# Two more steps in the size ramp of a channel shuffle: 4, 8, 16, 24, 32, then eleven tiles of 38 KB, 10 KB last

## The chip, the cores and the metric

The kernel runs on one core of a Trainium2 chip. The time is device microseconds (us) of that core for one execution. Most executions agree within 0.3%. A run is classed slow when it lies over 1.5% above the fastest run of the same kernel; only the other runs, classed fast, are compared. The profile is one execution. Its span, the time between its first and its last recorded instruction, is about 1.8 us shorter than the time of the same run. All sizes of tiles below are in KB for each of the 128 partitions: a "38 KB tile" is 128 rows of 38 KB, 4,864 KB in all.

## The reference

```python
x = np.random.randn(16, 64, 64, 256).astype(np.float32)   # 67.1 MB
groups = 8

def reference(x, groups):
    batch, h, w, c = x.shape
    x = x.reshape(batch, h, w, groups, c // groups)
    x = x.transpose(0, 1, 2, 4, 3)          # swap the two halves of the channel index
    return x.reshape(batch, h, w, c)
```

It is a permutation inside each group of 256 channels. Nothing is calculated: 67.11 MB are read and 67.11 MB are written.

## The kernel before

The 512 KB that each partition handles are cut into tiles. A tile is loaded in one DMA issued by SyncE, permuted by one copy on VectorE (DVE), and stored in one DMA issued by ScalarE. There are three input and two output buffers, so the copy of tile k waits until the store of tile k-2 has landed, and the load of tile k+3 is issued when the copy of tile k is done.

```python
_SIZES = [4, 8, 16] + [38] * 12 + [28]
_IN_BUFS = 3
_OUT_BUFS = 2
# ... (setting up, pools)
    for q in _SIZES:
        in_tile = in_pool.tile([P, biggest * c], F32, name="in_tile")
        nc.sync.dma_start(out=in_tile[:, : q * c], in_=rows(x_flat, first, q))
        out_tile = out_pool.tile([P, biggest * c], F32, name="out_tile")
        nc.vector.tensor_copy(
            out=out_tile[:, : q * c].rearrange("p (i j g) -> p i j g", j=CPG, g=G),
            in_=in_tile[:, : q * c].rearrange("p (i g j) -> p i j g", g=G, j=CPG),
        )
        nc.scalar.dma_start(out=rows(out_flat, first, q), in_=out_tile[:, : q * c])
        first += P * q
```

## Time and profile before

| | before |
|---|---|
| time, median of 3 runs (range) | 316.21 us (316.15 to 316.38) |
| span of the profiled run | 314.7 us |
| bytes moved | 134.22 MB, 427 GB/s over the span |
| load queue, store queue: share of the 16 DMA engines | 49.8%, 49.4% |
| DVE busy | 119.2 us (38%) |

The table says at once that transfers, not copies, fill the time. The view of the waits gives the opposite impression if it is read alone (columns: who waited for what, us in total, times, longest):

```profile
DVE out_tile L49 <- DMA out_dram<-out_tile: 175.9, 14, 14.6
```

DVE waits 176 us for stores to free an output buffer.

### The profile page before, as it was taken

What the parts mean: (1) busy time and instruction counts of PE and PEld (TensorE: products, weight loads), DVE (VectorE), ACT (ScalarE), POOL (GpSimd) and SP (SyncE); (2) the same over time, 40 slices, a digit from 0 to 9 for tenths busy, and PEclk for the clock granted to TensorE, in tenths of its full rate; (3) what the DMA queues carried; (4) which work ended last, traced back from release to release, by engine and by line L of the source; (5) the groups of instructions that cost most, each with busy time, mean ns of one, the idle gap of its engine ahead of it and who ended that gap; (6) DMA issues with size and microseconds to landing.
All of it is one profiled execution on the core that took longest, in us unless ns stands there. A gap on an engine that the chain in (4) does not pass through costs nothing.

```text
span 314.7 us, 133 instructions
## 1 busy us (share of the span) xinstructions
DVE 119.2 (38%) x16; POOL 0.2 (0%) x4
## 2 busy tenths in 40 slices
DVE  3040645505506407407308209109109019046620
POOL 0000000000000000000000000000000000000000
DMA  8999999999999999999999999999999999999997
GB/s 308 452 398 454 413 419 466 396 475 396 455 415 445 425 430 440 425 445 415 455 396 470 401 465 406 460 411 460 411 460 411 460 411 455 428 395 454 455 418 306
DMA packets 4608, 134.22 MB, mean 427 GB/s; under 512 B 512, under 2 KB 512, under 8 KB 768
## 3 DMA queue, kind: packets, MB, share of 16 engines
q1 hardware_dynamic: 2304, 67.11, 49.8%
q10 hardware_dynamic: 2304, 67.11, 49.4%
HBM read 67.11 MB, written 67.11 MB: 427 GB/s over the span
## 4 chain that ended last, share of the span: by engine, by line
DMA 75%; DVE 20%; issue 0%; SPq 0%; DVEq 0%
DMA out_dram<-out_tile 74%; DVE out_tile L49 20%; DMA in_tile<-in_x_dram 2%; SPq L47 0%; DVEq L49 0%
## 5 line engine op out<-in xcount | busy, mean ns | idle before, releaser
L49 DVE COPY out_tile<-in_tile 128x9728 f32<-128x9728 f32 (+4 forms) x16 | 119.2, 7449 | 181.4 <-DMA out_dram<-out_tile 175.9
L71 POOL MEMSET const-bfloat16-1.0<- 128x1 bf16 x1 | 0.1, 102 | 0.0
L71 POOL MEMSET const-uint8-127<- 128x1 uint8 x1 | 0.1, 102 | 0.0
L71 POOL MEMSET const-float32-1.0<- 128x1 f32 x1 | 0.1, 99 | 0.0
L71 POOL MEMSET const-float32-0.0<- 128x1 f32 x1 | 0.1, 98 | 0.2 <-issue 0.2
## 6 DMA issues: line engine op xcount, KB each, us to landing
in_tile<-in_x_dram SPq DMA_DIRECT2D x12, 4864.0 KB, 46.8
out_dram<-out_tile ACTq DMA_DIRECT2D x12, 4864.0 KB, 37.0
in_tile<-in_x_dram SPq DMA_DIRECT2D x1, 3584.0 KB, 43.8
out_dram<-out_tile ACTq DMA_DIRECT2D x1, 3584.0 KB, 13.3
in_tile<-in_x_dram SPq DMA_DIRECT2D x1, 2048.0 KB, 11.0
out_dram<-out_tile ACTq DMA_DIRECT2D x1, 2048.0 KB, 26.7
in_tile<-in_x_dram SPq DMA_DIRECT2D x1, 1024.0 KB, 5.4
out_dram<-out_tile ACTq DMA_DIRECT2D x1, 1024.0 KB, 25.8
```

The lines of the kernel that those rows point to most:

```text
L49: nc.vector.tensor_copy(out=out_tile[:, : q * c].rearrange("p (i j g) -> p i j g", j=CPG, g=G), in_=in_tile[:, : q * c].rearrange("p (i g ...
L71: nc = _bacc.Bacc("TRN2", target_bir_lowering=False, num_devices=1)
```

## The change

The intent is a smoother start: between the tile of 16 KB and those of 38 KB come steps of 24 and 32 KB, so that small stores do not have to share the DMA engines with loads of 38 KB, and output buffers come free sooner. The last tile shrinks from 28 to 10 KB, which also shortens the last copy and the last store.

```diff
-_SIZES = [4, 8, 16] + [38] * 12 + [28]
+_SIZES = [4, 8, 16, 24, 32] + [38] * 11 + [10]
```

## The prediction

> **What bounds the kernel now.** I read the page first (shares of the span, the 40 slices, the DMA queues), then the chain that ended last, the timeline of the copies, and last a table of windows cut at the starts of the copies. The page says that only one engine computes, and that it works little more than a third of the time, while the DMA engines are busy in every slice but the first and the last:
>
> ```profile
> span 314.7 us, 133 instructions
> DVE 119.2 (38%) x16; POOL 0.2 (0%) x4
> ...
> DMA  8999999999999999999999999999999999999997
> ...
> q1 hardware_dynamic: 2304, 67.11, 49.8%
> q10 hardware_dynamic: 2304, 67.11, 49.4%
> HBM read 67.11 MB, written 67.11 MB: 427 GB/s over the span
> ```
>
> Loads (q1) and stores (q10) take 49.8% and 49.4% of the sixteen engines' time: 99.2% together. The chain alone could mislead. It alternates a copy with the wait for a store that frees an output buffer, and so puts 20% of the span on DVE:
>
> ```profile
> DMA 75%; DVE 20%; issue 0%; SPq 0%; DVEq 0%
> ```
>
> A copy on this chain would cost time only if the DMA engines ran dry meanwhile. The windows say whether they do. Columns: window, its length, DVE busy, POOL busy, clock, DMA share, GB/s.
>
> ```profile
> 0.00:1.50 1.50, 0.00 (x0) 0.20 (x4) 1.00 0.00 0
> 1.50:5.00 3.50, 0.91 (x1) 0.00 (x0) 1.00 0.96 346
> 5.00:12.00 7.00, 2.19 (x2) 0.00 (x0) 1.00 0.99 394
> 12.00:20.36 8.36, 0.00 (x1) 0.00 (x0) 1.00 1.11 477
> 20.36:34.50 14.14, 3.90 (x2) 0.00 (x0) 1.00 0.98 415
> 34.50:51.03 16.53, 8.75 (x1) 0.00 (x0) 1.00 1.02 436
> ...
> 294.00:304.00 10.00, 6.54 (x1) 0.00 (x0) 1.00 1.01 436
> 304.00:311.00 7.00, 0.00 (x0) 0.00 (x0) 1.00 1.02 438
> 311.00:314.70 3.70, 0.00 (x0) 0.00 (x0) 1.00 0.38 163
> ```
>
> From 1.5 us on no window has a DMA share below 0.96 until the drain, not even the one that holds the last copy (294 to 304). Long packets are counted in one window whole, so 477 and 415 are one rate, about 438, seen twice. The packet records agree: the sum of all packets' times over 16 engines is 311.9 us, and the first packet starts at 1.8 us and the last ends at 313.6 us, which is 311.8 us. The end is even: the engines finish within about 1 us of one another. So the bound is the total DMA work, and DVE's 181 us of idle time cost nothing.
>
> **What the Trainium skill says.** "DMA: Bandwidth & Descriptors", Specifications, gives a fabric ceiling of 435 GB/s for the 16 engines; the trace agrees (433 to 436 in steady windows). By that figure 134.22 MB need at least 308.4 us, an estimate. The same page, Queues, rings and completion order, says that each DMA engine goes round robin between its queues packet by packet. The trace agrees, one load packet to one store packet, but the packet here is one partition's whole row, up to 38,912 bytes, far longer than the page's about 4 KB. "Perfetto Trace Analysis", DMA Optimizations, advises splitting DMAs where the DMA engines are generally idle; here they are not.
>
> **The change part by part.** It replaces one 38 KB tile and the last 28 KB tile by 24, 32 and 10 KB. Bytes, buffers and the first three tiles stay. (a) *Packet overhead.* The records give 159 ns for a 4 KB packet and 1439 ns for 38 KB: slope (1439 - 159)/34,816 B = 0.0368 ns per byte (27.2 GB/s an engine), intercept about 8 ns. Each engine serves 8 rows of a tile in each queue, so one more tile is 16 more packets, 16 x 8 = 0.13 us, and two completion packets of 9 ns: **+0.15 us** on the path. (b) *Copies.* 1083 ns at 4 KB and 8802 ns at 38 KB give 0.227 us per KB plus 0.175 us: 24, 32 and 10 KB cost 5.6, 7.4 and 2.4 us. One more copy adds 0.2 us to DVE's total, beside DMA work. (c) *The ramp.* A store's time is 8 of its packets and 8 load packets, by the alternation. This explains the copies' starts, as copy k waits for store k-2:
>
> ```profile
> 20.36 3.90 DVE L49 COPY out_tile<-in_tile 128x4096 f32<-128x4096 f32 x1 [11.75 <-DMA out_dram<-out_tile]
> 34.50 8.75 DVE L49 COPY out_tile<-in_tile 128x9728 f32<-128x9728 f32 x1 [10.24 <-DMA out_dram<-out_tile]
> 51.03 8.75 DVE L49 COPY out_tile<-in_tile 128x9728 f32<-128x9728 f32 x1 [7.78 <-DMA out_dram<-out_tile]
> ...
> 294.01 6.54 DVE L49 COPY out_tile<-in_tile 128x7168 f32<-128x7168 f32 x1 [5.95 <-DMA out_dram<-out_tile]
> ```
>
> The 8 KB store beside 38 KB loads: 8 x (0.31 + 1.44) = 14.0 us, seen 34.50 - 20.36 = 14.1. The 16 KB one: 8 x (0.61 + 1.44) = 16.4, seen 16.5. With 24 and 32 KB loads beside the small stores these come free sooner. When copy k starts, about 4.7 of the 8 packets of load k+1 are done (worked out in the steady part from the last load's end); I keep that, since the first three tiles stay. Then the third copy starts 4.7 x (1.44 - 0.91) = 2.5 us earlier, at **17.9 us**. The 8 KB store takes 8 x 0.31 + 3.3 x 0.91 + 4.7 x 1.21 = 11.2, so the 24 KB copy starts at **29.1**; the 16 KB store 4.9 + 3.3 x 1.21 + 4.7 x 1.44 = 15.7, so the 32 KB copy at **44.8**; the 24 KB store 8 x (0.91 + 1.44) = 18.8, to 63.6; the 32 KB store 21.2, to 84.8. From there 23.0 us a step, as now. None of this removes DMA work: what a store takes sooner, a load takes later, and both queues stay filled (at 32 us the loads issued by then are 122 KB a partition and the stores 28 KB, 150 x 0.301 = 45 us of work). So the ramp is worth **0**. (d) *The tail.* Eight full steps after 84.8 end at 268.8, where the last but two copy starts; the next store runs beside 3.3 load packets of 38 KB and 4.7 of 10 KB (0.385 us): 11.5 + 4.8 + 1.8 = 18.1, to 286.9. There the last 38 KB copy starts (8.8 us), while the store before it takes 11.5 + 3.3 x 0.385 = 12.8 us, to 299.7. The copy is done at 295.7, 4 us ahead; its store needs about 1 us to start (the first load: issued at 0.73, first packet at 1.8), so no gap. Then 11.5 us for that store and 8 x 0.385 = 3.1 for the 10 KB one: 314.3 us. The same sum for the kernel before gives 294.0 + 11.5 + 8.5 = 314.0. So the tail is worth **0** as well. Sum: +0.15 by (a), +0.3 by the schedule, which carries its rounding. On 316.21 us that makes 316.4.
>
> **The rivals.** *The ramp pays.* DVE idles 11.75 and 10.24 us before the copies at 20.36 and 34.50, and this shrinks. For it: 413 GB/s over the first 60 us against 434 later is a loss of 60 x (1 - 413/434) = 2.9 us. Against it: 1.8 us of that pass before the first packet, and the rest is mostly stretched packets of the first three loads, which stay. At best 1 us: 315.2. *The shorter tail pays.* Were the last copy and store a serial tail, 18 KB less would save 18 x 0.227 + 18 x 0.301 = 9.5 us, and the time would be 306.7. Against it: the windows from 294 to 311 run at 436 and 438 GB/s, and 306.7 lies under the 308.4 of the ceiling. *A gap in the tail.* The last 38 KB copy is now hidden behind one 12.8 us store without long loads beside it; an engine that runs 2 us ahead has about 1 us left. If the store's start takes 3 or 4 us, as the first store's did (issued at 5.2, first packet at about 9.5, with load packets ahead of it), engines stand still for 1 to 2 us: 317.4 to 318.4. I give it one chance in ten.
>
> **Range and chances.** The three runs before lie within 0.23 us. Below, some of the ramp's 1 us could come back: 315.6. Above, a small gap or another ordering: 317.2. A change of 2% is 6.3 us; nothing but a serial tail could give it, and only a starved stage could take it: faster 0.005, same 0.985, slower 0.01.
>
> **What would show each step.** Right: 4,896 packets instead of 4,608, DVE busy 119.4 us; copies at 17.9, 29.1, 44.8 and then 23.0 us apart, the last at about 299.7; no window from 1.5 to 311 us under a DMA share of 0.95; a span of 314.8 to 315.0. Wrong: a DMA slice under 9 inside the span, the last store starting after the one before it had ended, or an end of the DMA work before 313 us, which would mean that the kernel before held idle DMA time that I did not see.

## The result, and the profile after

The changed kernel takes 316.9 us (median of six runs, 316.23 to 317.26), the kernel before, run on the same chips in the same rounds, 316.4 us (six runs, 316.15 to 317.14). A ratio is the mean time of one kernel's fast runs over the mean of the other's fast runs of the same rounds, so it is not quite the ratio of the medians. Here it is 1.0011, with a 95% interval from 0.9996 to 1.0026: the same time. The median lies in the predicted range of 315.6 to 317.2 us, around 316.4.

The page of the changed kernel:

```profile
span 315.2 us, 139 instructions
DVE 119.6 (38%) x17; POOL 0.2 (0%) x4
DMA  8999999999999999999999999999999999999996
...
q1 hardware_dynamic: 2448, 67.11, 49.7%
q10 hardware_dynamic: 2448, 67.11, 49.3%
```

The DMA engines are busy in every slice but the first and the last, as before, and the two queues again fill 99.0% of the sixteen engines' time. There are 288 packets more, 144 in each queue: 128 rows of the extra tile and 16 completion packets.

The timeline of the copies that the change moved (start us, duration us, then the copy, and in brackets how long DVE had been idle and what ended it):

```profile
17.73 3.89 DVE L49 COPY out_tile<-in_tile 128x4096 f32<-128x4096 f32 x1 [9.14 <-DMA out_dram<-out_tile]
29.10 5.71 DVE L49 COPY out_tile<-in_tile 128x6144 f32<-128x6144 f32 x1 [7.49 <-DMA out_dram<-out_tile]
45.18 7.46 DVE L49 COPY out_tile<-in_tile 128x8192 f32<-128x8192 f32 x1 [10.37 <-DMA out_dram<-out_tile]
63.92 8.85 DVE L49 COPY out_tile<-in_tile 128x9728 f32<-128x9728 f32 x1 [11.28 <-DMA out_dram<-out_tile]
...
287.22 8.82 DVE L49 COPY out_tile<-in_tile 128x9728 f32<-128x9728 f32 x1 [8.81 <-DMA out_dram<-out_tile]
299.91 2.48 DVE L49 COPY out_tile<-in_tile 128x2560 f32<-128x2560 f32 x1 [3.86 <-DMA out_dram<-out_tile]
```

The third copy starts at 17.73 us instead of 20.36: the ramp did become quicker for DVE. It is worth nothing, and the windows say why (window, length, DVE busy, POOL busy, clock, DMA share, GB/s):

```profile
12.00:20.36 8.36, 2.63 (x1) 0.00 (x0) 1.00 1.06 445
20.36:34.50 14.14, 6.65 (x2) 0.00 (x0) 1.00 0.98 420
34.50:51.03 16.53, 6.16 (x2) 0.00 (x0) 1.00 1.02 436
294.00:304.00 10.00, 4.52 (x2) 0.00 (x0) 1.00 1.01 436
```

In the same windows as those shown for the kernel before, DVE now works 15.4 us between 12 and 51 us instead of 12.7 (the sums of the column), but the DMA engines move the same within what this count can tell: rate times length gives 16.9 MB after and 17.1 MB before, and one row of 38 KB on each of the 16 engines, counted whole in one window or the next, is 0.6 MB. They are fully loaded before and after. What a store gained, a load lost.

Where did the half microsecond between the two spans (314.7 and 315.2) go? The packet records of the trace, which hold start, duration and size of each packet and from which the shares above are summed, give this: all data packets together take 311.89 us on the mean of 16 engines before and 312.01 after (the completion packets of 9 ns add 0.29 and 0.31 us); the first packet starts 1.73 us after the first instruction in both; the last one ends at 313.53 before and at 313.90 after. So 0.12 us is packet work, 0.25 us is unevenness at the start and at the end (0.42 us of idle DMA time after 312 us before, 0.56 after), and the rest comes after the last packet. This is no more than the spread of the changed kernel's own runs, 1 us, so I do not read more into it. (The prediction put the first and last packet at 1.8 and 313.6; counted from the first instruction they are at 1.73 and 313.53. The difference, 311.8, is the same.) Such sums run a little high: most packets start 2 to 5 ns before the packet ahead of them on the same engine ends, which makes about 1 us in a whole run. So a sum of 311.9 us in a stretch of 311.8 us does not exclude about half a microsecond of idle time, most of it in the drain.

### The profile page after: what moved, and what is told of

It reads as the page before. It is cut to its first block, busy times and chain, and to the rows that moved or that the text cites. A ratio compares the mean times of both kernels' runs of the same rounds, so it can differ in the third digit from the quotient of the medians.

```text
span 315.2 us, 139 instructions
## 1 busy us (share of the span) xinstructions
DVE 119.6 (38%) x17; POOL 0.2 (0%) x4
## 2 busy tenths in 40 slices
DMA packets 4896, 134.22 MB, mean 426 GB/s; under 512 B 544, under 2 KB 544, under 8 KB 800
## 3 DMA queue, kind: packets, MB, share of 16 engines
q10 hardware_dynamic: 2448, 67.11, 49.3%
## 4 chain that ended last, share of the span: by engine, by line
DMA 77%; DVE 19%; issue 0%; DVEq 0%
DMA out_dram<-out_tile 76%; DVE out_tile L49 19%; DMA in_tile<-in_x_dram 1%; DVEq L49 0%
## 5 line engine op out<-in xcount | busy, mean ns | idle before, releaser
L49 DVE COPY out_tile<-in_tile 128x9728 f32<-128x9728 f32 (+6 forms) x17 | 119.6, 7034 | 182.8 <-DMA out_dram<-out_tile 177.3
```

What stands on the lines that cost most here:

```text
L49: nc.vector.tensor_copy(out=out_tile[:, : q * c].rearrange("p (i j g) -> p i j g", j=CPG, g=G), in_=in_tile[:, : q * c].rearrange("p (i g ...
```

## The experiments

Twelve kernels were run, all against the kernel before on the same chip. The first three take the change apart and overdo it.

### The ramp alone, the tail alone

```diff
-_SIZES = [4, 8, 16, 24, 32] + [38] * 11 + [10]
+_SIZES = [4, 8, 16, 24, 32] + [38] * 10 + [30, 18]   # ramp only
+_SIZES = [4, 8, 16] + [38] * 12 + [18, 10]           # tail only
```

> The new ramp (4, 8, 16, 24, 32) with a tail of 30 and 18 KB instead of the 10 KB tail. My theory: one tile more than before, plus 0.15 us, ratio 1.000 to 1.002. Rival (ramp and tail both act and cancel, the ramp gains up to 1 us): 315.3 us, ratio 0.997.

> The old ramp (4, 8, 16) with twelve of 38 KB, then 18 and 10: the short tail alone. My theory: one tile more, plus 0.15 us, ratio 1.000 to 1.002. Rival (ramp and tail cancel): the short tail costs what the ramp gained, ratio 1.003 or more; or the short tail gains, ratio under 0.997.

Measured: the ramp alone 316.37 us, ratio 0.9993 (0.9979 to 1.0007); the tail alone 316.94 us, ratio 1.0007 (0.9993 to 1.0021). Both are the same as before. Neither part moves by more than about 0.7 us, so a gain and a loss of 1 us that cancel are excluded; smaller ones are not. The ratio of the ramp stays above the 0.997 of its rival, and that of the tail under 1.003.

### No ramp at all

```diff
+_SIZES = [38] * 13 + [18]
```

> No ramp at all: thirteen tiles of 38 KB and one of 18. My theory (the sum of DMA work is the bound, the ramp is worth nothing): two tiles fewer than the kernel before, 2 x 0.15 = 0.3 us less packet work, so 316.0 us against 316.3, ratio 0.998 to 1.001, although the first copy starts only at about 13 us instead of 4. Rival (the ramp pays, because the first store starts sooner): the first store comes some 17 us later, and several us of that should be seen, 320 us or more; ratio over 1.01.

Measured: 347.92 us (346.69 to 348.82), ratio 1.0973. My expectation was wrong by 32 us. The rival said "320 or more", but its reason (the first store comes 17 us later) does not carry 32 us either, as the windows show:

```profile
100.00:200.00 100.00, 35.37 (x4) 0.00 (x0) 1.00 0.99 413
200.00:285.00 85.00, 26.69 (x3) 0.00 (x0) 1.00 1.00 401
285.00:300.00 15.00, 8.78 (x1) 0.00 (x0) 1.00 0.75 319
300.00:312.00 12.00, 0.00 (x0) 0.00 (x0) 1.00 0.77 332
312.00:347.00 35.00, 13.06 (x2) 0.00 (x0) 1.00 0.57 245
```

There are two losses, and neither is at the start. In mid-run the DMA engines are fully busy, yet move 413 and 401 GB/s where the kernel before moves 429 to 434: busy, but slower. Two windows of the kernel before:

```profile
100.00:150.00 50.00, 21.78 (x3) 0.00 (x0) 1.00 1.00 434
200.00:250.00 50.00, 17.63 (x2) 0.00 (x0) 1.00 0.99 429
```

The packet records show it: from 36 us on the 38 KB packets of the store queue that are stretched come mostly in groups of three, and take up to 2.4 us instead of 1.44. The records name no engine; that these are three engines of the sixteen follows if one takes each packet to start where the packet ahead of it on its engine ends. Load packets are stretched too, after the start mostly between 195 and 255 us. All data packets together take 323.0 us an engine instead of 311.9; of these 11 us, 6.6 are in the stores and 4.5 in the loads. Then, from 285 us on, part of the engines have run out of work while the late ones still load, and the share falls to 0.75 and 0.57. The first loss is 11 us, and idle time about 20 us more.

### Many small tiles

```diff
+_SIZES = [16] * 32     # tiles16
+_SIZES = [8] * 64      # tiles8
```

> 32 tiles of 16 KB, no ramp, 16 tiles more than the kernel before. My theory (a tile costs 16 packets of 8 ns and two completions of 9 ns on every engine, about 0.15 us, and nothing else): 16 x 0.15 = 2.4 us over the kernel before, 318.8 us, ratio 1.0075 (1.006 to 1.009). Rival 1 (a tile costs a fixed completion latency of 1 to 2 us, which the queues do not hide): 330 us or more. Rival 2, after the run without a ramp (whatever makes a start without smaller first tiles slow acts at any size): 330 us or more, with packets well over their shortest time.

> 64 tiles of 8 KB. My theory: 48 more tiles, 48 x 0.15 = 7.1 us, 323.5 us, ratio 1.022 (1.020 to 1.026); a store lasts 8 x (0.31 + 0.31) = 5 us and hides a copy of 2.0 us and about 1 us of start. Rival (at this size the waits are no longer hidden): 330 us or more, with a DMA share clearly under 0.97 in the middle windows.

Measured: with 32 tiles 319.44 us, ratio 1.0083 (1.0064 to 1.0102), inside the expected 1.006 to 1.009. The data packets' sum is 314.47 us, 2.58 us over the 311.89 of before, for 16 more tiles: 0.16 us a tile where part (a) of the prediction had 0.13, and 0.18 with the completion packets where it had 0.15. Its span also holds 1.5 us of idle DMA time between 300 and 312 us. That the range was still met is in part luck: the sums run high by the overlap of 2 to 5 ns a packet, which for 288 more packets on each engine is about 1 us, and the idle time makes up for it. By my estimate from these numbers a tile costs about 0.12 us. So this is also a kernel without a ramp, and it is not slow: what hurt the run without a ramp is not the missing ramp as such.

With 64 tiles the expectation failed: 389.89 and 394.18 us in the two fast runs, ratio 1.24. The profile fell in a run that was slow (397 us), so what follows describes that run; that the fast runs lose their time in the same way is not shown:

```profile
span 395.4 us, 421 instructions
q1 hardware_dynamic: 9216, 67.11, 49.6%
q10 hardware_dynamic: 9216, 67.11, 40.2%
```

The loads' packets take 49.6% of 395.4, or 196 us, where 64 tiles of 8 packets of 0.309 us need 158; the stores take 159, their minimum. And about 10% of the time the DMA engines are idle. In that run the stores keep their cost per packet; the loads get slower, and waits show through.

### The last two tiles swapped

```diff
-_SIZES = [4, 8, 16, 24, 32] + [38] * 11 + [10]
+_SIZES = [4, 8, 16, 24, 32] + [38] * 10 + [10, 38]
```

> The changed kernel with its last two tiles swapped: ten of 38 KB, then 10, then 38 last. Same tiles, same bytes, same number of packets. My theory says that a gap opens here: the last copy (8.8 us) starts when the store two before it has landed, while the 10 KB store in between lasts only 8 x 0.385 = 3.1 us; with about 0.5 us of landing and 1.4 us of start the DMA engines stand still for 10.7 - 3.1 = 7.6 us: 7 to 8.5 us over the changed kernel, 324 to 325.5 us. Rival (only bytes and packets count, order does not): the changed kernel's time, 316.7.

Measured: 324.46 us (324.42 to 324.74), ratio 1.0245 (1.0229 to 1.026), within the expected 324 to 325.5. The gap is where it was expected (windows of the swapped kernel, and its last copy):

```profile
300.00:305.00 5.00, 4.66 (x1) 0.00 (x0) 1.00 0.34 143
305.00:310.00 5.00, 4.18 (x1) 0.00 (x0) 1.00 0.00 0
310.00:315.00 5.00, 0.00 (x0) 0.00 (x0) 1.00 1.16 498
```

```profile
300.35 8.83 DVE L49 COPY out_tile<-in_tile 128x9728 f32<-128x9728 f32 x1 [14.15 <-DMA out_dram<-out_tile]
```

The copy runs from 300.35 to 309.2 us, and the DMA engines have nothing left from about 303 to 310 us; the records put their idle time between 300 and 312 us at 8.2 us on the mean. (The start of the last store, for which I had taken 1.4 us, is 0.9 us here: its first packet comes at 310.06. The engines' uneven end makes up for the difference, so the size was met partly by luck.) So the order of the same tiles can cost 8 us, and the rule by which the prediction found no gap in the changed tail also finds this one.

### The copy done twice

```diff
-        nc.vector.tensor_copy( ... )
+        for _ in range(2 if k < len(_SIZES) - 3 else 1):    # copy_twice_13
+        for _ in range(2 if k == len(_SIZES) - 2 else 1):   # copy_twice_late
+            nc.vector.tensor_copy( ... )
```

> The changed kernel with the copy done twice in all tiles but the last three (same result). DVE's busy time goes from 119.6 to about 218 us. My theory (copies lie beside DMA work; a doubled copy of 17.6 us plus 1.4 us of start still fits into a step of 23 us): the changed kernel's time within 0.5 us. Rival (the chain's 19% on DVE is time on the path): every second copy of the chain grows by 4 to 9 us, some 50 us more, 365 us.

> The changed kernel with the copy done twice in the last 38 KB tile alone (the last but one tile). It measures the slack of the tail. The copy starts at about 287.2 us and takes 17.7, so its store's first packet comes at about 306.3 with 1.4 us of start, while the store before it ends at about 299.5: a gap of 6.8 us; 6 to 7.5 us over the changed kernel, 322.5 to 324 us; so the single copy has about 2 us to spare. Rival (no slack, the changed tail already stands still): the whole 8.8 us more, 325.5.

With fourteen of the seventeen copies doubled the median is 316.40 us; the three fast runs lie between 316.27 and 316.52, ratio 0.9987 (0.9969 to 1.0005); a fourth run of 331.54 us was slow and is left out. The page:

```profile
span 314.5 us, 153 instructions
DVE 219.6 (70%) x31; POOL 0.2 (0%) x4
DMA 62%; DVE 34%; issue 0%; DVEq 0%
```

100 us more of DVE work cost nothing, although the view of the chain now puts 34% of the span on DVE instead of 19%. Those copies are not what sets the time: they lie beside DMA work.

With only the last 38 KB copy doubled the time is 323.05 us (322.41 to 323.44), ratio 1.0201 (1.0182 to 1.022), inside the expected 322.5 to 324 us. Against the kernel before that is 0.0201 x 316.5 = 6.4 us for 8.8 us of extra copy; against the changed kernel's own 316.9, from another session, it is 6.2 us. So about 2.5 us of slack stood in the changed tail, and the remainder is visible time.

### Why does a start with big tiles hurt?

Three kernels were to tell whether a late first store, or the addresses of 38 KB tiles, stretch the packets.

```diff
+_SIZES = [4] + [38] * 13 + [14]     # one_step
+_SIZES = [16] + [38] * 13 + [2]     # first16
+_SIZES = [36] * 14 + [8]            # no_ramp36
```

> A ramp of one step: 4 KB, then thirteen of 38 KB, then 14. After the run without a ramp (348 us, three DMA engines out of step and their store packets stretched from 1.44 to 2.2 us). Theory A (the stretch comes from stores that start late, when 38 KB loads have run alone for 26 us): the first store is issued at 5 us here as in the kernel before, so no stretch, 316.2 us with one tile fewer, ratio 0.999 to 1.002. Theory B (each step of a ramp must be small: 38 KB loads beside a 4 KB store put engines out of step): over 325 us.

> First tile of 16 KB, then thirteen of 38 KB, 2 KB last. The first store can be issued at about 11 us, between the 5 of the changed kernel and the 24 of the run without a ramp. Theory A (a late first store is what hurts): a loss between the two, 318 to 335 us. Rival (only tile bases at multiples of 38 KB rows, as in the run without a ramp, are bad): 316.3 us.

> No ramp, but tiles of 36 KB: fourteen of 36, then 8. Theory A (late first store): slow as with 38 KB, 335 us or more, with store packets of a few engines stretched over their shortest time. Rival (the addresses of 38 KB tiles without an offset are bad): 316.4 us, no stretched packets after the first 30 us.

Measured: with one step of 4 KB 329.03 us, ratio 1.0396 (1.0363 to 1.0428). The first store is issued at 5.19 us, as early as in the kernel before, and yet:

```profile
span 327.5 us, 127 instructions
DMA  8999999999999999999999999999999999999996
...
q10 hardware_dynamic: 2160, 67.11, 50.9%
q1 hardware_dynamic: 2160, 67.11, 48.0%
```

No slice is idle; the store queue's packets take 50.9% of 327.5, or 166.7 us, against 49.4% of 314.7, or 155.5 us, before: 11.2 us of the 12.6 lost. The load queue's take 157.2 and 156.7 us. So store packets are stretched from about 40 us to the end of the stage in which loads and stores are mixed. Since all 38 KB tiles here begin 4 KB a partition further on than in the run without a ramp, the unshifted addresses of that run are not needed for a loss. With a first tile of 16 KB, whose store is issued only at 12.47 us, the time is 318.54 us (316.97 to 319.29), ratio 1.0054 (1.0019 to 1.0089), and its profile, of the fastest run (316.97 us), has no store packet of 38 KB over 1.47 us between 20 and 300 us:

```profile
q10 hardware_dynamic: 2160, 67.11, 49.3%
```

That is 49.3% of a span of 315.2 us, 155.4 us. The three other runs, 317.9 to 319.3 us, have no profile, so their 1 to 2 us are not explained, and the median lies just inside the 318 to 335 us that the theory of the late first store had expected. What decides against this theory is one_step, with an early store and slow, beside the profiled run of first16, with a later store and fast: **the theory of the late first store falls**. With 36 KB tiles two runs were at 318.2 and 318.7 us, ratio 1.0057, and two at 343.5 and 343.8 were slow, the profile among them. The fast runs do not repeat the loss of the 38 KB tiles; I draw nothing from the slow ones.

The records suggested another cause. In the slow kernels the loads were some 76 to 81 KB a partition ahead of the stores when packets were stretched, in most clean runs less or more. (This fits the run without a ramp only up to about 120 us: counted from its records, on the mean of the engines, the loads are 96 to 111 KB ahead at 150 to 250 us, and its stores are still stretched.) The last run kept one_step's instructions, sizes, order and waits, and only stored each 38 KB tile one tile further on, so that the result is wrong:

```diff
+        at = first
+        if q == biggest:      # the last of these goes to the place of the first
+            at = first + P * q if first + P * q + P * q <= P * (4 + 13 * 38) else P * 4
-        nc.scalar.dma_start(out=rows(out_flat, first, q), in_=out_tile[:, : q * c])
+        nc.scalar.dma_start(out=rows(out_flat, at, q), in_=out_tile[:, : q * c])
```

> The run with one step (4, then thirteen of 38, 14), in which a mean store packet of 38 KB took 0.13 us more than its shortest time all along, with each 38 KB tile stored one tile further on in the output (wrong result on purpose; same instructions, sizes, order and waits). In the three slow runs the loads were 76 to 81 KB a partition ahead of the stores when store packets were stretched; clean runs lay at 42, 66 to 71 and 87 to 114. Stored one tile on, the distance between the addresses that are read and written at one time falls by 38 KB a partition, to about 40, as in the clean run with 16 KB tiles. Theory D (the distance of the addresses in memory stretches the packets): no stretch, 316.2 us. Rival (the order and phase of the packets on the engines do it, whatever the addresses): 329 us, stretched as before.

Measured: 328.88 us (328.02 to 329.64), ratio 1.0351 (1.0265 to 1.0437), and the page gives the same picture:

```profile
span 327.9 us, 127 instructions
q10 hardware_dynamic: 2160, 67.11, 50.8%
```

The stretch is the same with another distance between the addresses: the theory that a lead of 76 to 81 KB does it falls as well. It was one other distance, though. One tile is 4,864 KB, 19 times 256 KB, so an effect of addresses that repeats every 256 KB would survive this test; it is not tested. What else is left is how the packets of the two queues come to lie against each other on the engines. Its simplest form, that packets are stretched when all engines store at once, does not fit the traces: between 40 and 280 us at least 14 of the 16 engines store at the same time for 42% of the time in copy_twice_13, where a 38 KB store packet takes 1.44 us on the mean, and for 37% in one_step, where it takes 1.57. Nor is it shown that the two slow kernels have one cause: in one_step 87% of these store packets take over 1.48 us and the loads hardly take longer, in the run without a ramp 24% do, and loads are stretched too. No run here shows the mechanism, and **it stays open**.

## Why the prediction was right

**The bound.** The sum of the DMA work set the time. It is shown by both sides: 100 us more of copies cost nothing, and a tail order that lets the DMA engines run dry for 8.2 us cost 8 us.

**(a) Packet overhead, +0.15 us.** 4,896 packets came, and the sum of the data packets rose by 0.12 us for the 0.13 calculated (0.14 for 0.15 with the completion packets). The 16 more tiles of tiles16 raised it by 0.16 us each.

**(b) Copies.** 5.71, 7.46 and 2.48 us were measured for 5.6, 7.4 and 2.4; DVE's total is 119.6 us for 119.4.

**(c) The ramp, 0.** The copies started at 17.73, 29.10, 45.18, 63.92 and 85.10 us for 17.9, 29.1, 44.8, 63.6 and 84.8. So the rule of one load packet to one store packet describes the schedule within 0.4 us. The ramp alone measured 0.9993. The rival that promised 1 us from the quicker ramp has no support.

**(d) The tail, 0.** The last two copies started at 287.22 and 299.91 us for 286.9 and 299.7. The slack that I put at 4 us less 1 us of start, 3 us, measured about 2.5 us, so the rival of a gap was nearer than "4 us ahead" sounds. The 9.5 us of the serial tail did not come: there was no serial tail.

**What was not right.** Two signs failed. A window from 1.5 us on under a share of 0.95 would not come, I wrote, and 1.5 to 5.0 us has 0.91; the difference lies in the first loads, is 0.2 us, and is in the half microsecond above. And the span was to be 314.8 to 315.0 us; that of the profiled run is 315.2. The sum in the prediction is also wrong as it is written: 316.21 + 0.15 + 0.3 is 316.66, not 316.4. Both lie in the range, and the runs of one kernel spread by 1 us, so no run tells them apart. (Two smaller slips: 308.4 us comes from 435.2 GB/s, with the 435 of the text it is 308.5; and one steady window of the kernel before, 74 to 97 us, had 426 GB/s, not 433 to 436.)

More important is a premise of (c) that was true by luck of the sizes, not by the argument: that each packet takes its shortest time. It holds in the kernel before and after, but not with 38 KB tiles from the start, or behind a single tile of 4 KB: there 31 and 12.6 us are lost. My sentence that the ramp is worth 0 holds for the two added steps. Taking away the ramp that was there already cost 31 us, though other starts without it, 32 tiles of 16 KB or one first tile of 16 KB, cost under 1%; I learned this only from a run that I had expected to be equal.

## What to carry to other kernels

Where, as here, the two DMA queues together fill 99% of the engines' time, expect that moving copies or making output buffers free sooner only changes who goes first; look for packets over their shortest time and for stretches in which the engines run dry, and check a tail by comparing each copy with the store that lies beside it. A chain of waits that names the compute engine is not proof that it is on the path: doubling its work in one run is. And a schedule that looks neutral by bytes may not be: measure a kernel with bigger first tiles before trusting that the ramp is decoration.

## What the Trainium skill lacked or had wrong

- "DMA: Bandwidth & Descriptors", Queues, rings and completion order, and SWDGE vs HWDGE vs iDMA: they describe packets of some 9 to 17 descriptors and preferably up to 4096 B. Here a packet of the profile was one row of up to 38,912 B (1439 ns), and the alternation of the two queues at this grain decides how long a small store lasts: 14.1 us for an 8 KB tile beside 38 KB loads, 11.4 us beside 24 and 32 KB.
- The same page, Measured: it advises 1 MiB or more a DMA for at least 75% of peak. The tiles of 1 MiB (8 KB a partition) with loads and stores mixed gave 346 and 342 GB/s over the spans of the two fast runs (388.1 and 392.4 us), 79% of the 435 GB/s, in agreement; tiles of 2 MiB gave 423 GB/s. The page has no figure for two mixed streams.
- No page read says that packets can be stretched for most of a run when only the sizes of the first tiles differ: store packets of 38 KB took up to 2.4 us instead of 1.44, and the time rose from 316 to 348 us (no ramp) and 329 us (one step). The cause is open.
- "VectorE: DVE Perf Modes", The perf-mode tier table: it gives 1227 ns for an fp32 copy of 2048 elements in SBUF. The permuting copy of 2048 elements took 2025 ns here; the table has no row for such a pattern. (The skill does have rates for streams that do not run over neighbouring words, for other operations; none for this copy.)
